# A hybrid-trunk step on one core: triangular inverse moved to POOL, pooling branch moved, state kept undecayed

## The chip, the cores and the metric

The kernel runs on one core of a Trainium2 chip. The metric is device time in microseconds (us) of one execution. The median of three executions of the kernel before is 1899.89 us (1899.71 to 1901.06).

The engines are named as in the profile: PE multiplies matrices (PEld is its weight load), DVE is the vector engine, ACT the scalar engine with its activation tables, POOL the third elementwise engine, whose queue also issues DMAs. SP issues DMAs.

## The reference, cut to what matters

One layer of a trunk, for 256 prompt tokens and 64 sample tokens together (NT = 320):

```
proj = rmsnorm(x) @ w_in            -> u_pool | u_rwkv | g_pool | g_rwkv
A = pool_mixer(u_pool)              # trailing means of 2/4/8/16 tokens minus the token, one 256x256 map for each of 4 groups, a scale
B = rwkv7_mix(u_rwkv, S0)           # token shift, then for each of 16 heads a state S (64 x 64), token by token:
    S = S*w_t + (S @ -kk_t) b_t^T + v_t k_t^T ;  y_t = S @ r_t
x += (sigmoid(g_pool)*(A @ proj_pool) + sigmoid(g_rwkv)*(B @ proj_rwkv)) @ w_out
x += SwiGLU(rmsnorm(x));   x += sigmoid(rmsnorm(x) @ w_ple_gate) * (p @ w_ple_proj);   final rmsnorm
```

It also returns the last row before the shift, the last 15 pooling rows and the final states S.

## The kernel before, in words

**Layout.** Channels lie on the 128 partitions, the 320 tokens along the free axis. Every weight product is made in three float32r products (`mm3`, L111: high times high, high times low, low times high). `unit` (L91) brings eight 128x128 weight tiles: SP loads `raw`, ACT casts it to `wh` (L98), DVE subtracts to `wl` (L100; its rows show L56, the line of the helper `TT`). The three tags have three slots each. `gemm` (L103) runs through units; its accumulators `acc` have two PSUM banks.

**Order.** The program is written in one order, and a planner sets the order of each engine's queue when the kernel is built, by priorities and its own estimates of durations; on the chip every queue runs in that fixed order. Weight units have a raised priority (L94).

**Stages.** At the start (L189 to L336) come the small projection `pp`, the first norm and three narrow tiles (`low`, L289). Then come four groups (`group`, L423), one for every four heads, and after each group some `fill`s (L171): gemms that no group needs (the pooling input `d_u` and the gates `d_gate`, sent to DRAM). `FILLS` (L38) gives 5, 4, 4 and 22 of the 40. They are what PE has to do while a group's chain of small steps runs. After the last group comes the pooling branch (`pool_load`, `pool_diff`, `pool_mix`, L341 to L383), five more fills (L714), `acc_pa` (A times proj_pool), and then `acc_pb`, `acc_o`, the feed-forward `acc_fg`, `acc_fu` and `acc_fd`, `acc_pg` and the final norm.

**One group.** Six gemms `acc_q`, each shifted by a token (`shift`, L159): DVE multiplies into `rp`, in which every chunk of 64 tokens has a column ahead of it; two copies on POOL (L161, L162) fill that column, a third (L163) keeps the last row, ACT scales, DVE adds. The six tiles are scaled by accumulated decays into `ar` and `bk`; keys are normalized by `rsqrt_tp` (L693: Sqrt on ACT, reciprocal on DVE, a Newton step). Products of `bk` and `ar`, masked, are `mg`. For every chunk and head the kernel needs the inverse of a 64x64 unit triangular matrix. Its two 32x32 diagonal blocks, for all chunks and heads, go through DRAM (`dF`) into `xb`, 40 blocks on 40 partitions, and are inverted by 30 steps of two DVE instructions (L565 to L569):

```
for s in range(1, 31):
    n = 31 - s
    mul(tm, xb[:, 0:s, s:s + 1].broadcast_to([40, s, n]), xb[:, s:s + 1, s + 1:32].broadcast_to([40, s, n]))
    TT(xb[:, 0:s, s + 1:32], xb[:, 0:s, s + 1:32], tm, ALU.add)
```

DVE adds 1 on the diagonal, ACT makes a transposed copy `xbt` of 20 blocks (L572), both go through DRAM into `X` and `tz`, and PE makes the block below the diagonal (`pz`, `px`). Then the chunks go in four rounds (L621): PE reads the state (`ra`, L613), applies `X` (`pu`), makes the chunk's contribution `ps_s` (L642); DVE adds the old state and multiplies by the chunk's decay `pcs` (L651, L653), which gives `sbd`, the state that the next round's `ra` reads. Group norm and gate follow (L666 to L691), and the result goes to DRAM (`d_yb`).

Of the kernel before, what the change touches and what calls it, by code (L numbers as in the profile page):

```python
# [13 lines left out]
ALU = mybir.AluOpType  # L14
# [23 lines left out]
FILLS = (5, 4, 4, 22)  # L38
# [10 lines left out]
def trunk_step(ctx: ExitStack, tc: tile.TileContext, xT, pT, cols, w_low, s0T, poolpast, cst, maskc, invc,  # L49
# [139 lines left out]
    with tc.tile_pool(name="start", bufs=1) as st:  # L189
# [99 lines left out]
        def low(q, a=None):  # L289
            rp = st.tile([P, NCH, C + 1], F32, tag="rp", name="rp0", bufs=2)  # L290
            xs = xstd.rearrange("p (c t) -> p c t", c=NCH)
# [6 lines left out]
            ac = a.rearrange("p (c t) -> p c t", c=NCH)  # L298
            if q == 2:
# [38 lines left out]

    ZL = PAST + T_P + PAST + T_S
# [10 lines left out]
    def pool_diff(gi, z):  # L350
# [12 lines left out]
        t16 = rk.tile([P, 2, 16], F32, tag="tm", name="t16")  # L363
# [10 lines left out]
    def pool_mix(gi, dh, dl):  # L374
        h, l = unit(w_poolw[gi], 4, f"pw{gi}")
        for i in range(2):
# [5 lines left out]
            act.activation(yah[:, j, :], a, AF.Copy, scale=col(C_PS + j))  # L382
            stt(yal[j], a, col(C_PS + j), f(yah[:, j, :]), ALU.mult, ALU.subtract)  # L383
# [9 lines left out]
    with tc.tile_pool(name="rk", bufs=1) as rk:  # L393

        def shift_tile(q, out):
# [27 lines left out]
        def group(g):  # L423
# [109 lines left out]

            bt = rk.tile([P, 2 * NCH, P], F32, tag="bt", name="bt")
# [68 lines left out]
            sbd_in = rk.tile([P, 2, P], F32, tag="sbd", name="sbd_in", bufs=4)  # L603
# [16 lines left out]
            states = {4: sbd_in, 0: None}  # L620
            for cs in ((4, 0), (1,), (2,), (3,)):  # L621
# [326 lines left out]
```

## Time and profile before

| | us |
|---|---|
| median of three executions | 1899.89 |
| the profiled execution, its own time | 1900.61 |
| its span, first to last instruction | 1898.7 |
| PE busy in the span | 1863.8 |
| DVE / ACT / POOL busy | 1120.1 / 798.6 / 138.7 |
| mean granted clock of PE | 0.993 of full speed |

The span and what lies around it (1.9 us) make the execution's own time. A clock of 1.00 is 2.4 GHz, of 0.50 is 1.2 GHz. Busy time doesn't say what an engine waited for: the views of the rows below do.

### The profile page before, as it was taken

What the parts mean: (1) busy time and instruction counts of PE and PEld (TensorE: products, weight loads), DVE (VectorE), ACT (ScalarE), POOL (GpSimd) and SP (SyncE); (2) the same over time, 40 slices, a digit from 0 to 9 for tenths busy, and PEclk for the clock granted to TensorE, in tenths of its full rate; (3) what the DMA queues carried; (4) which work ended last, traced back from release to release, by engine and by line L of the source; (5) the groups of instructions that cost most, each with busy time, mean ns of one, the idle gap of its engine ahead of it and who ended that gap; (6) DMA issues with size and microseconds to landing.
All of it is one profiled execution on the core that took longest, in us unless ns stands there. A gap on an engine that the chain in (4) does not pass through costs nothing.

```text
span 1898.7 us, 32757 instructions
## 1 busy us (share of the span) xinstructions
PE 1863.8 (98%) x13444; PEld 1838.0 (97%) x13444; DVE 1120.1 (59%) x1674; ACT 798.6 (42%) x1060; POOL 138.7 (7%) x282
## 2 busy tenths in 40 slices
PE   8999999899999999999999999999999999999997
PEld 7999999799989999999999999999999999999997
DVE  7676976877857465555454554444545554445655
ACT  6554536464455334443333333223333333333543
POOL 0110222202310112000000000000000000000000
PEclk9999999899999999999999999999999999999998
DMA  7554544345545657444444444554444444555553
GB/s 274 168 170 150 167 147 148 105 161 181 169 138 189 199 191 233 146 152 148 151 150 149 152 147 148 146 151 156 153 146 154 146 154 143 152 146 150 169 170 117
DMA packets 95349, 302.99 MB, mean 160 GB/s; under 512 B 12224, under 2 KB 23248, under 8 KB 95200
## 3 DMA queue, kind: packets, MB, share of 16 engines
q1 hardware_dynamic: 78336, 271.71, 44.3%
q0 software_dynamic: 6816, 17.39, 3.0%
q10 hardware_dynamic: 10048, 11.80, 1.7%
q8 instruction: 106, 1.74, 0.4%
q14 instruction: 43, 0.35, 0.1%
HBM read 284.12 MB, written 16.73 MB: 158 GB/s over the span
## 4 chain that ended last, share of the span: by engine, by line
PE 95%; DVE 3%; DMA 1%; issue 1%; ACT 0%; SPq 0%; DVEq 0%; ACTq 0%
PE acc_fd L115 5%; PE acc_fu L116 5%; PE acc_fg L116 5%; PE acc_fg L115 5%; PE acc_fg L117 5%; PE acc_fu L117 5%; PE acc_fd L116 5%; PE acc_fu L115 5%; PE acc_fd L117 5%; PE acc_f L115 4%; PE acc_f L116 4%; PE acc_f L117 4%; PE acc_q L117 3%; PE acc_q L115 3%; PE acc_q L116 3%; PE acc_pg L115 2%
## 5 line engine op out<-in xcount | busy, mean ns | idle before, releaser
L116 PE MATMUL acc_fg<-nl,wh_fg 128*128 128x320 f32 x704 | 217.8, 309 | 0.0
L115 PE MATMUL acc_fg<-nh,wh_fg 128*128 128x320 f32 x704 | 217.6, 309 | 0.1
L115 PE MATMUL acc_fu<-nh,wh_fu 128*128 128x320 f32 x704 | 217.5, 309 | 0.0
L117 PE MATMUL acc_fu<-nh,wl_fu 128*128 128x320 f32 x704 | 217.5, 309 | 0.0
L116 PE MATMUL acc_fu<-nl,wh_fu 128*128 128x320 f32 x704 | 217.5, 309 | 0.0
L117 PE MATMUL acc_fg<-nh,wl_fg 128*128 128x320 f32 x704 | 217.5, 309 | 0.0
L56 DVE TENSOR_TENSOR wl_fd<-raw_fd,wh_fd 128x1024 fp32r<-128x1024 f32 (+1 forms) x96 | 109.1, 1136 | 151.7 <-ACT wh_fd L98 151.7
L98 ACT CAST wh_fd<-raw_fd 128x1024 fp32r<-128x1024 f32 (+1 forms) x96 | 94.1, 980 | 203.1 <-PE acc_fd L116 162.4
L98 ACT CAST wh_fg<-raw_fg 128x1024 fp32r<-128x1024 f32 x88 | 92.5, 1051 | 199.1 <-PE acc_fg L116 98.7
L98 ACT CAST wh_fu<-raw_fu 128x1024 fp32r<-128x1024 f32 x88 | 92.5, 1052 | 190.8 <-PE acc_fu L116 103.4
L56 DVE TENSOR_TENSOR wl_fg<-raw_fg,wh_fg 128x1024 fp32r<-128x1024 f32 x88 | 107.8, 1225 | 105.3 <-ACT wh_fg L98 105.3
L115 PE MATMUL acc_f<-xh,wh_f 128*128 128x320 f32 x512 | 160.8, 314 | 1.7 <-ACT wh_f L98 1.7
L116 PE MATMUL acc_f<-xl,wh_f 128*128 128x320 f32 x512 | 160.6, 314 | 0.0
L117 PE MATMUL acc_f<-xh,wl_f 128*128 128x320 f32 x512 | 159.5, 312 | 0.8 <-DVE wl_f L56 0.8
L115 PE MATMUL acc_fd<-hh,wh_fd 128*128 128x320 f32 x512 | 158.2, 309 | 0.0
L116 PE MATMUL acc_fd<-hl,wh_fd 128*128 128x320 f32 x512 | 158.2, 309 | 0.0
L117 PE MATMUL acc_fd<-hh,wl_fd 128*128 128x320 f32 x512 | 158.2, 309 | 0.0
L56 DVE TENSOR_TENSOR wl_fu<-raw_fu,wh_fu 128x1024 fp32r<-128x1024 f32 x88 | 107.8, 1226 | 83.9 <-ACT wh_fu L98 83.9
L115 PEld LDWEIGHTS acc_fg<-nh,wh_fg 128*128 128x128 f32 x704 | 132.2, 188 | 0.3 <-issue 0.3
L116 PEld LDWEIGHTS acc_fg<-nl,wh_fg 128*128 128x128 f32 x704 | 132.2, 188 | 0.1
L117 PEld LDWEIGHTS acc_fg<-nh,wl_fg 128*128 128x128 f32 x704 | 132.2, 188 | 0.1
L116 PEld LDWEIGHTS acc_fu<-nl,wh_fu 128*128 128x128 f32 x704 | 132.2, 188 | 0.0
(490 smaller groups left out, 4913.0 us busy)
## 6 DMA issues: line engine op xcount, KB each, us to landing
raw_fg<-in_w_gate SPq DMA_DIRECT2D x88, 512.0 KB, 3.7
raw_fu<-in_w_up SPq DMA_DIRECT2D x88, 512.0 KB, 3.7
raw_f<-in_w_in SPq DMA_DIRECT2D x64, 512.0 KB, 4.0
raw_fd<-in_w_down SPq DMA_DIRECT2D x64, 512.0 KB, 3.6
raw_q<-in_w_in SPq DMA_DIRECT2D x48, 512.0 KB, 3.9
raw_o<-in_w_out SPq DMA_DIRECT2D x32, 512.0 KB, 3.7
raw_pg<-in_w_pg SPq DMA_DIRECT2D x32, 512.0 KB, 3.9
raw_fd<-in_w_down SPq DMA_DIRECT2D x32, 384.0 KB, 3.5
```

The source lines that it names most:

```text
L56: return vec.tensor_tensor(out=out, in0=a, in1=b, op=op)
L98: act.copy(h, raw)
L115: pe.matmul(out=acc, lhsT=hs[i], rhs=xh, start=first and i == 0, stop=False)
L116: pe.matmul(out=acc, lhsT=hs[i], rhs=xl, start=False, stop=False)
L117: pe.matmul(out=acc, lhsT=ls[i], rhs=xh, start=False, stop=last and i == n - 1)
```

## The change

- **Inverse.** The 60 instructions of a group's inverse, the diagonal and the transposed copy go to POOL.
- **Pooling.** It is written directly behind the last group and ahead of its fills, of which there are now 27 (none is left for afterwards). Its weights no longer go through `unit`: POOL loads them into slots of the tag `tp`. Its output goes to DRAM (`d_ya`) and is read back by POOL, cast by ACT and split by DVE ahead of `acc_pa`.
- **Shift.** `rp` has no column ahead of a chunk; the two copies on POOL go, and a second, two-column DVE instruction makes the first token of either request.
- **Undecayed state.** The next round reads the state without `pcs`; `ar` of chunks 1 to 3 carries it instead (one POOL instruction for a group, `later`). DVE multiplies by `pcs` into `dec`, which the next round's addition reads.
- **Log norms.** In `rsqrt_tp` the reciprocal becomes Ln and Exp on ACT.
- **Start and end.** The four first matmuls on zeros write `acc` banks; the last norm's factor comes by another formula, one DVE instruction shorter; the output goes in nine pieces, the first two half as large.

```diff
-FILLS = (5, 4, 4, 22)
+FILLS = (5, 4, 4, 27)
...
     def shift(q, rp, t, out):
-        pool.tensor_copy(out=rp[:, 0:5:4, 0], in_=ssz[:, q, :])
-        pool.tensor_copy(out=rp[:, 1:4, 0], in_=rp[:, 0:3, C])
-        pool.tensor_copy(out=nshift[:, q, :], in_=rp[:, 3:5, C])
-        act.activation(t, rp[:, :, 1:], AF.Copy, scale=omu[:, q:q + 1])
-        stt(out.rearrange("p (c t) -> p c t", c=NCH), rp[:, :, 0:C], col(C_MU + q), t, ALU.mult, ALU.add)
+        pool.tensor_copy(out=nshift[:, q, :], in_=rp[:, T_P - 1:NT:T_S])
+        act.activation(t, rp, AF.Copy, scale=omu[:, q:q + 1])
+        stt(out[:, 1:], rp[:, 0:NT - 1], col(C_MU + q), t[:, 1:], ALU.mult, ALU.add)
+        stt(out[:, 0:T_P + 1:T_P], ssz[:, q, :], col(C_MU + q), t[:, 0:T_P + 1:T_P], ALU.mult, ALU.add)
...
-            w = small("warm_ps", [P, NT])
+            w = acc_tile("warm_ps")
...
     def pool_mix(gi, dh, dl):
-        h, l = unit(w_poolw[gi], 4, f"pw{gi}")
+        raw = rf.tile([P, 4 * P], F32, tag="tp", name="raw_pw", bufs=6)
+        pool.dma_start(out=raw, in_=w_poolw[gi])
+        h = rf.tile([P, 4 * P], F32R, tag="tp", name="wh_pw", bufs=6)
+        act.copy(h, raw)
+        l = rf.tile([P, 4 * P], F32R, tag="tp", name="wl_pw", bufs=6)
+        TT(l, raw, f(h), ALU.subtract)
...
-            act.activation(yah[:, j, :], a, AF.Copy, scale=col(C_PS + j))
-            stt(yal[j], a, col(C_PS + j), f(yah[:, j, :]), ALU.mult, ALU.subtract)
+            o = sp.tile([P, NT], F32, tag="gate", name="pool_o", bufs=2)
+            act.activation(o, a, AF.Copy, scale=col(C_PS + j))
+            act.dma_start(out=d_ya[j], in_=o)
...
+            later = ar[:, :, 1:4].rearrange("p j c s t -> p j c (s t)")
+            pool.tensor_tensor(out=later, in0=later, in1=pcs[:, :, 0:3].unsqueeze(3).broadcast_to([P, 2, 3, P]),
+                               op=ALU.mult)
...
-                mul(tm, xb[:, 0:s, s:s + 1].broadcast_to([40, s, n]), xb[:, s:s + 1, s + 1:32].broadcast_to([40, s, n]))
-                TT(xb[:, 0:s, s + 1:32], xb[:, 0:s, s + 1:32], tm, ALU.add)
+                pool.tensor_tensor(out=tm, in0=xb[:, 0:s, s:s + 1].broadcast_to([40, s, n]),
+                                   in1=xb[:, s:s + 1, s + 1:32].broadcast_to([40, s, n]), op=ALU.mult)
+                pool.tensor_tensor(out=xb[:, 0:s, s + 1:32], in0=xb[:, 0:s, s + 1:32], in1=tm, op=ALU.add)
...
-            vec.tensor_scalar(out=diag, in0=diag, scalar1=1.0, scalar2=None, op0=ALU.add)
-            act.copy(xbt, xb[0:20].rearrange("u s t -> u t s"))
+            pool.tensor_scalar(out=diag, in0=diag, scalar1=1.0, scalar2=None, op0=ALU.add)
+            pool.tensor_copy(out=xbt, in_=xb[0:20].rearrange("u s t -> u t s"))
...
-                    for lo in halves:
-                        src = ps[lo, i]
-                        if states[c] is not None:
-                            TT(nxt[lo, :, lo], src, states[c][lo, :, lo], ALU.add)
-                            src = nxt[lo, :, lo]
-                        mul(nxt[lo, :, lo], src, pcs[lo, :, c:c + 1].broadcast_to([64, 2, C]))
+                    for lo, new_s in zip(halves, at):
+                        if states[c] is None:
+                            vec.tensor_copy(out=new_s, in_=ps[lo, i])
+                        else:
+                            old = sbd_in[lo, :, lo] if c == 4 else dec[c][lo]
+                            TT(new_s, ps[lo, i], old, ALU.add)
                     new[c] = nxt
+                    for lo, new_s in zip(halves, at):
+                        mul(dec[c + 1][lo], new_s, pcs[lo, :, c:c + 1].broadcast_to([64, 2, C]))
...
             act.activation(s, am, AF.Sqrt)
+            act.activation(s, s, AF.Ln)
             r = tp("r")
-            vec.reciprocal(out=r, in_=s)
+            act.activation(r, s, AF.Exp, scale=-1.0)
...
             group(g)
+            if g == 3:
+                for gi in range(4):
+                    pool_mix(gi, *pool_diff(gi, pool_load(gi)))
             fill(n)
...
-        for gi in range(4):
-            pool_mix(gi, *pool_diff(gi, pool_load(gi)))
+        for j in range(8):
+            yt = sp.tile([P, NT], F32, tag="gate", name="ya", bufs=2)
+            pool.dma_start(out=yt, in_=d_ya[j])
+            act.copy(yah[:, j, :], yt)
+            TT(yal[j], yt, f(yah[:, j, :]), ALU.subtract)
```

## Rows read from the trace of the kernel before

**Rows 1.** The page's first part: busy time, share of the span, instructions.

```profile
PE 1863.8 (98%) x13444; PEld 1838.0 (97%) x13444; DVE 1120.1 (59%) x1674; ACT 798.6 (42%) x1060; POOL 138.7 (7%) x282
```

**Rows 2.** Stretches: length, busy PE, PEld, DVE, ACT, POOL, granted clock, DMA share, GB/s.

```profile
20.00:40.00 20.00, 15.78 (x98) 14.10 (x96) 17.61 (x26) 12.31 (x21) 0.00 (x0) 1.00 0.82 278
...
340.00:360.00 20.00, 12.46 (x115) 11.41 (x115) 19.18 (x33) 7.43 (x14) 5.25 (x12) 0.74 0.35 109
...
349.00:360.00 11.00, 6.33 (x53) 5.92 (x54) 10.38 (x20) 3.18 (x7) 3.68 (x9) 0.53 0.21 73
...
556.00:578.00 22.00, 16.30 (x166) 13.50 (x166) 18.54 (x37) 10.24 (x21) 4.91 (x8) 1.00 0.34 106
...
578.00:582.00 4.00, 4.00 (x18) 4.00 (x19) 3.65 (x11) 2.64 (x5) 0.00 (x0) 0.57 0.47 154
```

**Rows 3.** Timeline around the first stall: start, duration, instruction, idle before and its releaser.

```profile
337.49 4.15 DVE L697 RECIPROCAL r<-s 128x640 f32<-128x640 f32 x1 [2.14 <-ACT s L695]
...
347.63 0.44 PE L613 MATMUL ra<-sbd,ar 128*64 128x128 f32 x4 [2.21 <-DVE sbd L56]
...
352.12 0.61 DVE L56 TENSOR_TENSOR sbd<-ps_s,sbd 64x128 f32<-64x128 f32 x2
...
354.89 0.60 DVE L56 TENSOR_TENSOR sbd<-sbd,pcs 64x128 f32<-64x128 f32 x2
...
355.63 0.69 PE L613 MATMUL ra<-sbd,ar 128*64 128x128 f32 x4 [4.20 <-DVE sbd L56]
```

**Rows 4.** Timeline around the second stall, SP's queue and PE.

```profile
535.71 13.89 SPq L96 DMA_DIRECT2D raw_pw<-in_w_poolw  x4
...
565.56 0.44 PE L613 MATMUL ra<-sbd,ar 128*64 128x128 f32 x4 [0.97 <-DVE sbd L56]
...
568.41 0.41 PE L115 MATMUL acc_f<-xh,wh_f 128*128 128x320 f32 x1 [0.61 <-ACT wh_f L98]
...
575.41 0.42 PE L115 MATMUL acc_f<-xh,wh_f 128*128 128x320 f32 x1 [1.11 <-ACT wh_f L98]
...
577.85 0.41 PE L117 MATMUL acc_f<-xh,wl_f 128*128 128x320 f32 x1 [0.75 <-DVE wl_f L56]
```

**Rows 5.** Groups of DVE instructions: busy in all, mean ns, idle before.

```profile
L56 DVE TENSOR_TENSOR tm<-xb 40x30 f32<-40x30 f32 (+14 forms) x120 | 38.3, 319 | 11.4 <-DMA xb<-dF 8.8
...
L697 DVE RECIPROCAL r<-s 128x640 f32<-128x640 f32 x4 | 16.6, 4149 | 3.6 <-ACT s L695 3.6
```

**Rows 6.** Stretches that hold the inverses of groups 1 and 3, tile xb alone: DVE, ACT, POOL.

```profile
257.00:295.00 38.00, 19.36 (x61) 1.24 (x1) 0.54 (x1) 1.00 0.42 137
...
467.00:509.00 42.00, 19.42 (x61) 1.93 (x1) 1.07 (x2) 1.00 0.45 143
```

**Rows 7.** POOL by groups, and POOL beside DVE in the timeline.

```profile
L161 POOL COPY rp<-ssz 128x2 f32<-128x2 f32 x27 | 16.0, 596 | 11.2 <-DVE ssz L267 4.8 <-DVE xv L62 2.9 <-DVE xb L56 2.2
L542 POOL MEMSET uv<- 64x1280 f32 x4 | 4.7, 1165 | 6.2 <-PE py_c L617 3.6 <-PE acc_q L117 2.5
...
219.47 3.94 POOL L161 COPY rp<-ssz 128x2 f32<-128x2 f32 x1
...
222.15 1.21 DVE L56 TENSOR_TENSOR wl_q<-raw_q,wh_q 128x1024 fp32r<-128x1024 f32 x1
223.57 0.60 DVE L62 SCALAR_TENSOR_TENSOR xr<-rp,ct,tsh 128x320 f32<-128x320 f32 x1 [0.21 <-POOL rp L162]
...
223.63 0.18 POOL L161 COPY rp<-ssz 128x2 f32<-128x2 f32 x1
```

**Rows 8.** Groups of ACT instructions.

```profile
L695 ACT ACT_TABLE_LOAD x4 | 5.1, 1283 | 2.9 <-DVE am L485 2.9
```

**Rows 9.** Timeline at the end, DVE.

```profile
1888.70 5.94 DVE L56 TENSOR_TENSOR X<-X,r_fin 128x640 f32<-128x640 f32 x8 [1.30 <-PE r_fin L859]
```

**Rows 10.** Tile acc_pa: duration min/median/max in ns, first and last start in us.

```profile
L115 PE MATMUL acc_pa<-yah,wh_pa x128: 306/308/314, 613.2 to 669.1; 128*128 128x320 f32 x128
```

**Rows 11.** DMA issues: number, KB each, median us from issue to landing.

```profile
gate<-d_gate POOLq DMA_DIRECT2D x32, 160.0 KB, 3.2
```

More of the change, by code (lines that the diff above doesn't have):

```diff
@@ L289, in low @@
         def low(q, a=None):
-            rp = st.tile([P, NCH, C + 1], F32, tag="rp", name="rp0", bufs=2)
-            xs = xstd.rearrange("p (c t) -> p c t", c=NCH)
+            rp = st.tile([P, NT], F32, tag="rp", name="rp0", bufs=2)
             if a is None:
@@ L297, in low @@
                     gemm(a, w_in[q], KD, f"t{q}", xs_in)
-            ac = a.rearrange("p (c t) -> p c t", c=NCH)
             if q == 2:
@@ L302, in low @@
                     act.copy(r3[32 * i:32 * i + 32], a[96:128])
-                TT(rp[0:96, :, 1:], ac[0:96], r3[0:96].rearrange("p (c t) -> p c t", c=NCH), ALU.add)
-                mul(rp[0:96, :, 1:], rp[0:96, :, 1:], xs[0:96])
-                mul(rp[96:128, :, 1:], ac[96:128], xs[96:128])
-            else:
-                mul(rp[:, :, 1:], ac, xs)
-            t = st.tile([P, NCH, C], F32, tag="tsh", name="tsh0", bufs=2)
+                TT(rp[0:96], a[0:96], r3[0:96], ALU.add)
+                mul(rp[0:96], rp[0:96], xstd[0:96])
+                mul(rp[96:128], a[96:128], xstd[96:128])
+            else:
+                mul(rp, a, xstd)
+            t = st.tile([P, NT], F32, tag="tsh", name="tsh0", bufs=2)
             out = st.tile([P, NT], F32, tag="xm0", name="xm0", bufs=2)
@@ L336, in trunk_step @@
         TT(t2s[64:96], t2[64:96], f(t2s[64:96]), ALU.subtract)
+    d_ya = dr.tile([8, P, NT], F32, name="d_ya")
     ZL = PAST + T_P + PAST + T_S
@@ L362, in pool_diff @@
         a, b = PAST, 2 * PAST + T_P
-        t16 = rk.tile([P, 2, 16], F32, tag="tm", name="t16")
+        t16 = rk.tile([P, 2, 16], F32, tag="t16", name="t16")
         mul(t16, cur[:, :, a:a + 16], iv[:, gi:gi + 1, :].broadcast_to([P, 2, 16]))
@@ L398, in shift_tile @@
             gemm(a, w_in[q], KD, f"q{q}", xs_in)
-            rp = rf.tile([P, NCH, C + 1], F32, tag="rp", name="rp", bufs=3)
-            mul(rp[:, :, 1:], a.rearrange("p (c t) -> p c t", c=NCH), xstd.rearrange("p (c t) -> p c t", c=NCH))
-            t = rf.tile([P, NCH, C], F32, tag="tsh", name="tsh", bufs=2)
+            rp = rf.tile([P, NT], F32, tag="rp", name="rp", bufs=3)
+            mul(rp, a, xstd)
+            t = rf.tile([P, NT], F32, tag="tsh", name="tsh", bufs=2)
             shift(q, rp, t, out)
@@ L602, in group @@
             ysb = rk.tile([P, NCH, 2, C], F32, tag="ysb", name="ysb")
-            sbd_in = rk.tile([P, 2, P], F32, tag="sbd", name="sbd_in", bufs=4)
+            sbd_in = rk.tile([P, 2, P], F32, tag="sbd", name="sbd_in", bufs=3)
             pool.memset(sbd_in, 0.0)
@@ L620, in group @@
             states = {4: sbd_in, 0: None}
+            dec = {}
             for cs in ((4, 0), (1,), (2,), (3,)):
@@ L851, in trunk_step @@
                       stop=src is sql and i == 2)
-    rc = fp.tile([P, 3], F32, name="rc")
-    rsqrt(fp, s, c_eps, [P, 3], "rsc", 3, rc)
+    rc = [fp.tile([P, 3], F32, tag="rsc", name="rsc", bufs=4) for _ in range(4)]
+    act.activation(rc[0], s, AF.Sqrt, bias=c_eps)
+    vec.reciprocal(out=rc[1], in_=rc[0])
+    stt(rc[2], s, c_eps, rc[1], ALU.add, ALU.mult)
+    TT(rc[2], rc[2], rc[0], ALU.add)
+    vec.reciprocal(out=rc[3], in_=rc[2])
     rr = small("r_fin", [P, 1, NT])
@@ L857, in trunk_step @@
         dg = fp.tile([P, P], F32, tag="dg", name="dg", bufs=3)
-        vec.tensor_scalar(out=dg, in0=ident, scalar1=rc[:, i:i + 1], scalar2=None, op0=ALU.mult)
+        vec.tensor_scalar(out=dg, in0=ident, scalar1=rc[3][:, i:i + 1], scalar2=2.0, op0=ALU.mult, op1=ALU.mult)
         pe.matmul(out=rr[:, 0, lo:t + P], lhsT=one_sq, rhs=dg[:, lo - t:], start=True, stop=True)
-    for m in range(0, KD, 2):
-        mul(X2[:, m:m + 2, :], X2[:, m:m + 2, :], rr.broadcast_to([P, 2, NT]))
-        nc.sync.dma_start(out=o_y[:, m:m + 2, :], in_=X2[:, m:m + 2, :])
+    for m, n in ((0, 1), (1, 1), (2, 2), (4, 2), (6, 2), (8, 2), (10, 2), (12, 2), (14, 2)):
+        mul(X2[:, m:m + n, :], X2[:, m:m + n, :], rr.broadcast_to([P, n, NT]))
+        nc.sync.dma_start(out=o_y[:, m:m + n, :], in_=X2[:, m:m + n, :])
 def kernel(**inputs):
```

13 lines of the change are left out of this document (10 added, 3 removed).

## The prediction

> **What bounds the kernel now.** The page's first part comes first: PE is busy in 98% of the span and every other engine in at most 59% [rows 1]. An edit that leaves PE's instructions alone, as this one does, can gain only where PE stands still or runs slowly. The table by stretches shows where: apart from the start and the end there are two places. From 340 to 360 PE is busy for 12.46 of 20 us, so it idles 7.5; in 349 to 360 its granted clock averages 0.53, so the 6.33 us that it was busy there held some 3.0 us too many. From 556 to 578 it idles 5.7, and in 578 to 582 its clock is 0.57, which costs another 1.7 [rows 2]. Together that is 17.9 us, 0.9% of the time, and nearly all that the middle of the kernel can give.
>
> The timeline says what ends these waits. In the first stall PE waits for the state: `ra` stands behind DVE for 2.21 and 4.20 us [rows 3]. A chain of two DVE steps leads there, the addition at 352.12 and the multiplication by the decay at 354.89; DVE is not slow in them, it has other work between and is busy for 19.18 of the 20 us [rows 2, 3]. Part of that backlog is a reciprocal of 4.15 us just before [rows 3]. In the second stall PE waits for the weights of fills, 0.61, 1.11 and 0.75 us, and again for the state, 0.97 [rows 4]. The weights are late because four pooling units, asked for by SP from 535.71 on [rows 4], lie in the three weight slots until their pooling tiles are ready.
>
> **The change, part by part.**
>
> *Undecayed state.* The multiplication leaves the way to `ra`. In the long wait PE could start when the addition ends, 352.12 + 0.61 = 352.73, and not at 355.63: 2.8 us. The short wait of 2.21 loses between the multiplications' own 0.6 and all of it; I take 1.4. The 0.97 of the second stall goes: 1.0. The instruction `later` on POOL has 768 elements on a partition. POOL's nearest row is a memset of 1280 elements in 1.165 us, 0.91 ns each [rows 7]: 0.7 us for one pass, 2.1 if its two reads and its write come in turn, hidden behind the inverse's DMAs, which PE's state reads wait for anyway; exposed, at most 4 x 2.1 = 8.4.
>
> *Inverse off DVE.* 120 pairs leave DVE; one half took 38.3 us [rows 5], so both about 77, and with the reciprocals' 16.6 DVE is rid of 93 us in the stretch of the groups. What it is worth is only the backlog: the first stall's idle time less the two waits above, 7.5 - 2.8 - 1.4 = 3.3. I take half, 1.6; the ends are 0 and 3.3.
>
> *Inverse on POOL.* No row shows a POOL tensor_tensor. A step has on average the sum of s(31 - s) over 30 steps, 4960, divided by 30: 165 elements. A POOL copy of two elements takes 0.18 us undisturbed [rows 7], one pass over 165 elements by the memset 0.15. Low end: 0.18 + 0.15 = 0.33 us. High end: three passes, and every instruction waits as the copies L161 do on average (596 ns less 0.18): 0.18 + 0.45 + 0.42 = 1.05 us. Why they wait is plain at 219.47: a copy of two elements takes 3.94 us, DVE's subtraction from 222.15 on ends at 223.36, and the copy ends at 223.41 [rows 7]. I take two passes and half the wait, 0.18 + 0.30 + 0.21 = 0.69, because DVE will be emptier by 93 us. So an inverse takes 60 x 0.69 = 41 us, within 20 and 63. On DVE, between other work, it took at most 38 and 42 us in groups 1 and 3 [rows 6], and longer in groups 0 and 2. It is then no later than before, and fills cover it as they did. For what comes late I charge 1.5 us (ends 0 and 46, below).
>
> The Trainium skill has a rule against this part: the page SBUF — State Buffer, section Who interferes with whom, says that a DVE instruction with two SBUF inputs and a POOL instruction that reads SBUF exclude each other, and that the one that starts first holds the port for its whole length. The trace agrees for one direction, the copy of 3.94 us [rows 7]; for the other it has only a DVE wait of 0.21 us for a POOL copy that it needed [rows 7]. By that rule the term would be no gain from DVE's freed time, which is the second rival.
>
> *Queued behind the inverse on POOL:* the `nshift` copies, the loads of the gate, of `X` and `tz`, the states' stores, and the pooling's loads. A held `nshift` holds one of three `rp` buffers and then DVE and an `acc` bank; that costs PE only if POOL lets nothing through for the time of some five gemms. I count 0; if the cover goes, it is part of the slower case.
>
> *Transposed copy and diagonal.* 1024 elements in a row on POOL: one pass 0.9, two 1.9 us, plus a wait; ACT loses as much. The chain is as long as before: 0.
>
> *Shift.* 27 times two POOL copies go (L161 alone 16.0 us [rows 7]); 27 small DVE instructions come, each at most the 319 ns of an inverse step [rows 5], below 9 us in all, on an engine that gets 93 back: 0.
>
> *Log norms.* 4.15 us of DVE give way to two passes of ACT, each a fifth of that or less by the 0.74 us of a 128x640 DVE pass (5.94 for eight [rows 9]), and one or two table loads of 1.28 [rows 8]: 2.8 to 4.0 us. The chain is not longer, and the ACT time, at most 16 us, is under PE's gemms: 0.
>
> *The pooling branch* keeps its arithmetic, but its weights no longer take the fills' slots. The three waits go, 0.61 + 1.11 + 0.75 = 2.5 us. It gains a way through DRAM: eight stores, eight loads by POOL, eight casts and subtractions. Fills run until `acc_pa` starts at 613.2 [rows 10], so this is covered as long as the pooling ends some 20 us earlier; if not, see the third rival.
>
> *Clock.* In both stalls the clock fell to the lower level, 1.2 GHz, only behind several us of idle PE. If the waits shrink as above, 3.0 + 1.7 = 4.7 us come back; if half of them stay, none.
>
> *Start and end.* At the start DVE is busy for 17.61 of 20 us and ACT for 12.31 [rows 2]; the edits there take nothing off either: 0, within 1.3 either way. At the end one DVE instruction of about 0.2 goes, and the first store starts some 0.3 earlier because its multiplication is half as long (0.37 for 0.74 [rows 9]), one more piece is issued: -0.3, within -0.5 and +0.3.
>
> **The sum.** First stall 2.8 + 1.4 + 1.6 + 3.0 = 8.8; second 1.0 + 2.5 + 1.7 = 5.2; end 0.3; charged 1.5. The gain is 12.8 us on the profiled execution's 1900.6: 1887.8, rounded to 1888. That execution is 0.7 above the median of the runs shown, within what I round. This case's own range is 1883 to 1895.
>
> **The rivals.**
>
> 1. *POOL's inverse comes late, and PE stands before it (slower).* The place is `pz`, the first matmul that needs the inverse. PE's queue has a fixed order, so when POOL is slower than the planner thought, the gemms behind `pz` wait too. The price: at 0.90 us a step (two passes, the full mean wait) an inverse takes 54 us, 16 more than the 38 of group 1 and 12 more than the 42 of group 3 [rows 6]. 28 us against 14.3 gained: 1900.6 - 14.3 + 28 = 1914. It decides from (38 + 42 + 14.3) / 120 = 0.79 us a step. At the high end of 1.05 an inverse takes 63, 46 late in all, and the time is 1932. For it speaks that a POOL copy can wait 3.94 us; against it, that much of DVE's load is what goes away, and that groups 0 and 2 lived with longer inverses without a PE wait for them. The Trainium skill's GPSIMD Engine Reference, section Elementwise — side-by-side cycle accounting, measures a tensor_tensor there at 1.96 times DVE's time; by that estimate a step is 0.63 us, short of this point.
>
> 2. *The port gives DVE nothing back (the inverse moved in name only).* 240 steps of 0.69 are 166 us in which DVE's two-input work must wait, more than the 93 freed. The backlog stays and the clock falls again. What is left is 2.8 + 1.4 + 1.0 + 2.5 + 0.3 less 1.5: 6.5, so 1894. If the two waits for the state also come back behind other queued work, it is 1898.
>
> 3. *The pooling output comes late (no change).* The last fills end before `acc_pa` has its input. POOL's loads stand behind group 3's inverse, and with two buffers the eight loads go in four rounds of about 3.2 us [rows 11] and two passes of at most 0.74 [rows 9]: 4 x 4.7 = 19 us. If 13 of them lie open, it eats the gain: 1900.
>
> 4. *All of both stalls goes.* 7.5 + 3.0 + 5.7 + 1.7 + 0.5 = 18.4: 1882.
>
> **How the numbers follow.** Forecast 0.50; rival 1 0.21; rival 2 0.10, half of it on either side of the bound; rival 3 0.09; rival 4 0.10. A difference below 0.2%, 3.8 us, can hardly be told from none: faster is below 1896.1, slower above 1903.7. Faster 0.50 + 0.10 + 0.05 = 0.65; same 0.09 + 0.05 = 0.14; slower 0.21. The range reaches from 1879, somewhat below rival 4 (the start's 1.3 and a little), to 1910; it takes in rivals 2 to 4 and the lower part of rival 1, and leaves out the rest of it, some 0.14.
>
> **What would show it.** Right: no PE wait of over 1 us for `ra` behind DVE, no wait of fills for `wh_f` around the pooling, PE's clock at 1.00 throughout the groups, POOL's steps at 0.5 to 0.8 us from start to start, DVE some 90 us less busy. Wrong: PE waits for `pz` or `px` behind `tz` and `X` (rival 1); DVE's wl subtractions longer than 1.2 us and the first stall still there (rival 2); idle PE right before `acc_pa` (rival 3). A gain at the start or the end of more than 1.5 us would show a term that I set at nothing.

## The result, and the profile after

The changed kernel takes 1918.93 us in the median (1916.8 to 1920.03), the kernel before beside it 1900.43: a ratio of 1.0094, with a 95% interval of 1.0082 to 1.0107. It is slower by 18.5 us. The profiled execution of the changed kernel took 1918.91 us with a span of 1917.1, 18.4 us more than the span before. The page's first part:

```profile
PE 1869.1 (97%) x13444; PEld 1843.6 (96%) x13444; DVE 1077.1 (56%) x1461; ACT 811.1 (42%) x1083; POOL 311.4 (16%) x484
```

Against [rows 1] PE is busy 5.3 us longer and idle 13.1 us longer (1917.1 - 1869.1 = 48.0, before 1898.7 - 1863.8 = 34.9): together the 18.4 us. DVE is 43 us less busy, not 90. The waits of PE (line waited for, releaser; us in total, times, longest) name a wait that was not there before:

```profile
PE pz L596 <- DMA tzz<-dT: 15.3, 3, 7.1
PE acc_pw L115 <- ACT wh_pw L376: 4.0, 1, 4.0
```

The waits for `ra` of [rows 3, 4] are gone, and those of the fills too. The stretches (columns as in [rows 2]) show both stalls of before filled, and where the time went instead:

```profile
220.00:240.00 20.00, 13.93 (x157) 13.25 (x156) 9.39 (x14) 5.28 (x9) 4.98 (x7) 0.74 0.41 123
320.00:340.00 20.00, 12.88 (x151) 12.05 (x150) 7.82 (x10) 12.38 (x18) 4.09 (x8) 0.74 0.38 118
340.00:360.00 20.00, 20.00 (x194) 18.52 (x194) 15.90 (x29) 7.34 (x13) 2.56 (x6) 1.00 0.34 109
440.00:460.00 20.00, 17.89 (x245) 16.43 (x245) 16.75 (x28) 9.91 (x18) 6.84 (x12) 0.91 0.70 205
520.00:540.00 20.00, 16.02 (x99) 15.75 (x98) 10.50 (x15) 7.25 (x10) 15.53 (x29) 0.91 0.71 207
560.00:580.00 20.00, 20.00 (x195) 18.70 (x194) 12.60 (x26) 8.92 (x16) 2.64 (x5) 1.00 0.48 149
```

The four largest new stalls stand in place of two; over the stretches of the first two the granted clock averages 0.74. The timeline gives the first three their name. PE waits for the transposed inverse, in groups 0, 1 and 2:

```profile
228.79 1.28 PE L596 MATMUL pz<-tzz,mg 32*32 32x32 f32 x40 [6.07 <-DMA tzz<-dT]
...
329.03 1.28 PE L596 MATMUL pz<-tzz,mg 32*32 32x32 f32 x40 [7.12 <-DMA tzz<-dT]
...
443.29 0.82 PE L596 MATMUL pz<-tzz,mg 32*32 32x32 f32 x40 [2.11 <-DMA tzz<-dT]
```

One would say: POOL is slower than DVE. The tile `tm`, by which each of the four inverses can be followed (number; duration min/median/max in ns; first and last start in us), shows that this is only a part of it. First the kernel before, groups 0 to 3:

```profile
L56 DVE TENSOR_TENSOR tm<-xb x30: 182/342/401, 166.5 to 233.9; 40x30 f32<-40x30 f32 x2, 40x58 f32<-40x58 f32 x2, 40x84 f32<-40x84 f32 x2, 40x108 f32<-40x108 f32 x2
L56 DVE TENSOR_TENSOR tm<-xb x30: 183/338/401, 258.0 to 292.6; 40x30 f32<-40x30 f32 x2, 40x58 f32<-40x58 f32 x2, 40x84 f32<-40x84 f32 x2, 40x108 f32<-40x108 f32 x2
L56 DVE TENSOR_TENSOR tm<-xb x30: 182/324/399, 389.2 to 452.6; 40x30 f32<-40x30 f32 x2, 40x58 f32<-40x58 f32 x2, 40x84 f32<-40x84 f32 x2, 40x108 f32<-40x108 f32 x2
L56 DVE TENSOR_TENSOR tm<-xb x30: 182/342/400, 471.2 to 506.1; 40x30 f32<-40x30 f32 x2, 40x58 f32<-40x58 f32 x2, 40x84 f32<-40x84 f32 x2, 40x108 f32<-40x108 f32 x2
```

And the changed kernel:

```profile
L576 POOL TENSOR_TENSOR tm<-xb x30: 320/569/1634, 166.4 to 214.0; 40x30 f32<-40x30 f32 x2, 40x58 f32<-40x58 f32 x2, 40x84 f32<-40x84 f32 x2, 40x108 f32<-40x108 f32 x2
L576 POOL TENSOR_TENSOR tm<-xb x30: 250/599/1689, 263.7 to 317.0; 40x30 f32<-40x30 f32 x2, 40x58 f32<-40x58 f32 x2, 40x84 f32<-40x84 f32 x2, 40x108 f32<-40x108 f32 x2
L576 POOL TENSOR_TENSOR tm<-xb x30: 247/552/1602, 378.6 to 430.4; 40x30 f32<-40x30 f32 x2, 40x58 f32<-40x58 f32 x2, 40x84 f32<-40x84 f32 x2, 40x108 f32<-40x108 f32 x2
L576 POOL TENSOR_TENSOR tm<-xb x30: 226/568/1437, 475.6 to 524.0; 40x30 f32<-40x30 f32 x2, 40x58 f32<-40x58 f32 x2, 40x84 f32<-40x84 f32 x2, 40x108 f32<-40x108 f32 x2
```

From first to last start DVE took 67.4, 34.6, 63.4 and 34.9 us, 200 in all; POOL takes 47.6, 53.3, 51.8 and 48.4, 201 in all. So in groups 1 and 3 the inverse is 19 and 14 us longer than on DVE, in groups 0 and 2 it is 20 and 12 us *shorter*. Yet in group 0 PE now waits 6.07 us, where it waited for nothing. What also differs is PE's own queue. Counted in the two kernels' orders, between a group's last masked product and its `pz` there stood 552, 322, 529 and 335 gemm matmuls before, and 409, 398, 414 and 452 now. One takes 0.147 us from start to start, so the cover was 81, 47, 78 and 49 us and is 60, 59, 61 and 66. The order is set when the kernel is built; the planner's estimates are not on record, only the order that came of them.

Both sides together give the waits. In us from the start of a group's last masked product, to the landing of `tz` (the transposed inverse, `tzz` in the rows) and to PE's arrival at `pz`:

| group | `tz` there, before / now | PE at `pz`, before / now | PE waits now |
|---|---|---|---|
| 0 | 87.5 / 73.4 | 89.9 / 67.3 | 6.1 |
| 1 | 57.0 / 76.7 | 59.7 / 69.6 | 7.1 |
| 2 | 86.6 / 74.5 | 87.6 / 72.4 | 2.1 |
| 3 | 57.8 / 74.0 | 62.7 / 81.5 | none |

In groups 0 and 2 PE comes sooner by more than the inverse does; in group 1 the inverse comes later by more than PE. In group 0 the way out grew as well. These are the loads of `tz` there, before and after:

```profile
241.63 0.68 POOL L583 DMA_DIRECT2D tzz<-dT  x1
...
223.89 0.68 POOL L592 DMA_DIRECT2D tzz<-dT  x1
```

They landed 2.3 and 4.9 us after their issue, so from the start of the last step (233.9 and 214.0) to the landing it was 10.0 us and is 14.8. In groups 1 and 2 it went from 11.6 to 11.9 and from 11.6 to 12.9.

The last new stall, in 520 to 540, is the wait for `acc_pw`. The timeline shows its weights: POOL issues their load only near the end of group 3's inverse, behind which it was queued.

```profile
521.16 0.61 POOL L374 DMA_DIRECT2D raw_pw<-in_w_poolw  x1
...
525.53 0.42 PE L115 MATMUL acc_pw<-dh,wh_pw 128*128 128x320 f32 x1 [3.98 <-ACT wh_pw L376]
```

The groups of instructions (busy in all, mean ns of one, idle before) give the price of the steps, and what DVE paid:

```profile
L576 POOL TENSOR_TENSOR tm<-xb 40x30 f32<-40x30 f32 (+14 forms) x120 | 85.4, 712 | 19.8 <-DMA xb<-dF 11.2
L578 POOL TENSOR_TENSOR xb<-xb,tm 40x30 f32<-40x30 f32 (+14 forms) x120 | 83.7, 697 | 8.3
...
L56 DVE TENSOR_TENSOR wl_q<-raw_q,wh_q 128x1024 fp32r<-128x1024 f32 x48 | 62.3, 1298 | 38.4 <-ACT wh_q L98 38.2
```

A step's instruction is busy for 705 ns in the mean; the 60 of an inverse, with what POOL does between them, take 49.2, 53.9, 52.4 and 49.1 us to the end of the last one, 0.85 us each. DVE's subtraction for `wl_q` went from 1219 to 1298 ns in the mean.

### The profile page after: what moved, and what is told of

Same layout as the page of the kernel before. It is cut to its first block, busy times and chain, and to the rows that moved or that the text cites. A ratio compares the mean times of both kernels' runs of the same rounds, so it can differ in the third digit from the quotient of the medians.

```text
span 1917.1 us, 32767 instructions
## 1 busy us (share of the span) xinstructions
PE 1869.1 (97%) x13444; PEld 1843.6 (96%) x13444; DVE 1077.1 (56%) x1461; ACT 811.1 (42%) x1083; POOL 311.4 (16%) x484
## 4 chain that ended last, share of the span: by engine, by line
PE 81%; POOL 10%; DMA 3%; issue 2%; DVE 1%; ACT 1%; SPq 0%; ACTq 0%; DVEq 0%; POOLq 0%
PE acc_fd L116 5%; PE acc_fg L115 5%; PE acc_fg L117 5%; PE acc_fu L117 5%; PE acc_fu L115 5%; PE acc_fu L116 5%; PE acc_fg L116 5%; PE acc_fd L117 5%; PE acc_fd L115 5%; POOL tm L576 4%; POOL xb L578 4%; PE acc_pg L117 2%; PE acc_o L116 2%; PE acc_o L115 2%; PE acc_pg L116 2%
## 5 line engine op out<-in xcount | busy, mean ns | idle before, releaser
L854 POOL DMA_DIRECT2D pp<-d_pp x16 | 8.6, 538 | 1117.9 <-DVE gt L56 1117.1
```

Of the source, the lines that this page charges most:

```text
L854: pool.dma_start(out=pp, in_=d_pp[m])
```

## The experiments

Medians and ratios go against runs of the kernel before on the same chip (1899.85 to 1900.96 us in the median).

| run | what | us | ratio, 95% interval |
|---|---|---|---|
| e2_inv_only | before + inverse part | 1923.63 | 1.0121 [1.0106, 1.0136] |
| e4_micro | the steps by themselves, another program, one run | 256.15 | none |
| e5_pool_move | before + pooling move | 1906.7 | 1.003 [1.0018, 1.0042] |
| e7_undecayed | before + undecayed state | 1899.73 | 0.9996 [0.9987, 1.0005] |
| e10_log_norms | before + log norms | 1900.49 | 0.9998 [0.9988, 1.0007] |
| e1_inv_back | change - inverse part | 1907.69 | 1.0042 [1.0025, 1.0059] |
| e6_pool_back | change - inverse part - pooling move | 1904.69 | 1.0024 [1.0015, 1.0034] |
| e3_half | change, half the steps on DVE | 1901.64 | 1.0004 [0.9995, 1.0013] |
| e8_pz_late | change, `pz` later, spread | 1924.38 | 1.0122 [1.0107, 1.0137] |
| e9_pz_block | change, `pz` later in groups 0, 1 | 1912.34 | 1.0066 [1.0052, 1.0079] |
| e13_pz_all | change, `pz` later in all groups | 1904.73 | 1.0022 [1.0013, 1.0032] |
| e11_pool_early | before + pooling beside group 2 | 1895.88 | 0.9976 [0.9968, 0.9985] |
| e12_half_pool_early | e3_half + pooling beside group 2 | 1904.84 | 1.0024 [1.0015, 1.0033] |
| e14_no_inv_pool_early | e1_inv_back + pooling beside group 2 | 1898.41 | 1.0 [0.9987, 1.0013] |
| e15_early_undecayed | e11_pool_early + undecayed state | 1896.89 | 0.9987 [0.9978, 0.9996] |

### The inverse part alone, undone, and halved

```
e1 (on the change), e2 the other way round (on the kernel before):
-  pool.tensor_tensor(out=tm, ...); pool.tensor_tensor(out=xb[...], ...)
+  mul(tm, ...); TT(xb[...], ...)
-  pool.tensor_scalar(out=diag, ...); pool.tensor_copy(out=xbt, ...)
+  vec.tensor_scalar(out=diag, ...); act.copy(xbt, ...)
e3 (on the change): steps s <= 15 on POOL, the others, diag and xbt as in e1
```

> The changed kernel with the 60 steps of a group's inverse and the diagonal back on DVE and the transposed copy back on ACT; all other parts of the change stay. Theory (the inverse on POOL is ready later than PE's fixed order allows, so PE stands before pz in every group): the four waits for pz go, and what the other parts gain stays: 1883 to 1893 us. Rival (the loss comes from other parts: the pooling's loads on POOL's queue, the table loads of the log norms, a longer DVE): it stays above 1905 us.

> The kernel before with only the inverse, the diagonal and the transposed copy moved to POOL. Theory: PE waits for pz in most groups, and the time is 1912 to 1930 us, since the stalls of before are not mended either. Rival (other parts carry the loss): 1890 to 1903 us.

> The changed kernel with steps 1 to 15 of the inverse on POOL, steps 16 to 30 and the diagonal on DVE, the transposed copy on ACT. Theory: an inverse spends some 25 us on POOL and under 20 on DVE, PE's wait for pz falls to under 3 us a group, 1885 to 1900 us. Rival (the loss is not from the length of POOL's part): the same 1915 to 1921 us as the changed kernel.

The inverse part alone costs more than the whole change, 22.7 us (1923.63 against 1900.96). PE's waits in it:

```profile
PE pz L588 <- DMA tzz<-dT: 18.4, 3, 9.1
PE acc_f L115 <- ACT wh_f L98: 6.0, 3, 4.3
```

Its `pz` stands behind 399, 409, 414 and 452 gemm matmuls, nearly the cover of the changed kernel: the planner moves `pz` when the inverse alone becomes POOL's. With the inverse back (e1) the change is 11 us faster, but still 6.7 slower than before; the 1883 to 1893 that the theory gave were missed. There PE waits elsewhere:

```profile
PE acc_pa L115 <- ACT yah L738: 5.8, 4, 3.0
PE pz L595 <- DMA tzz<-dT: 2.8, 1, 2.8
```

So a second part costs something once the first is gone. Half the steps on each engine (e3) bring the time to that of before, just outside the expected 1885 to 1900, with one `pz` wait of 1.6 us left.

### The steps by themselves

> Not the computation: it only runs the 60 steps on POOL on zeros six times: alone, beside back-to-back DVE subtractions with two SBUF operands (128x1024), alone, beside such with one operand in PSUM, alone, beside DVE subtractions alternating with DVE reductions; the outputs are zeros. Theory (DVE's two-operand instructions keep POOL from reading): 33 to 42 us alone, 50 us or more beside the first kind until DVE is done, as alone beside the second, in between beside the third; DVE's subtractions get longer than 1.23 us only beside the first and the third kind. Rival (POOL is slow by itself): about 50 us in all six.

The six inverses did not meet DVE's work as planned: it ran beside the first three, and the last three ran alone. That answers the question too. The stretches are the first four inverses (length; busy DVE; busy POOL; clock; DMA); the last two are as the fourth:

```profile
7.30:67.60 60.30, 58.31 (x46) 55.62 (x60) 1.00 0.14 50
67.60:105.70 38.10, 37.04 (x33) 33.40 (x60) 1.00 0.00 0
105.70:150.90 45.20, 33.27 (x26) 40.44 (x61) 1.00 0.00 0
150.90:185.40 34.50, 0.00 (x0) 29.79 (x61) 1.00 0.00 0
```

Alone an inverse takes 34.5 us, 0.575 a step. The first three met mixtures, so the steps tell more. While subtractions of two SBUF tiles ran one after the other (11.7 to 57.5 us), POOL came through 30 steps, 1.53 us each from start to start, and a subtraction took 1.49 in the mean. Beside the same subtraction with one operand in PSUM, 18 steps of the same inverse took 0.52 each and 47 of the next 0.61, and the subtraction stayed at 1.22. The third inverse met alternating subtractions and one-input reductions for most of its time and took 45 us.

In the changed kernel an inverse takes 49 to 54. Its 240 instructions can be sorted by what DVE ran beside them: 74 beside nothing took 0.437 us in the mean (the same ones alone in e4: 0.434), 76 beside a weight subtraction 1.04 (alone 0.535), 90 beside other work of DVE 0.64 (alone 0.507). Of the 50.7 us by which all are longer than alone, 38.6 fall to those beside a weight subtraction. The Trainium skill's page SBUF — State Buffer, section Who interferes with whom, has the rule for this (a DVE instruction with two SBUF inputs and a POOL instruction that reads SBUF exclude each other); these runs agree, for both directions, with the 1.53 and 0.52 us of a step and the 1.49 and 1.22 of a subtraction.

### `pz` later in PE's order

```
e8:
+      with tc.high_priority(offset=(-1450, -1450, -1600, -1300)[g]):
           for u in range(10): for jj in range(2): pe.matmul(out=pz[...], ...)
e9, ahead of that loop, which stays as in the change:
+      for jj in range(2):
+          with tc.high_priority(offset=(-1500, -1450, -1650, -1300)[g]):
+              pe.matmul(out=pz[64 * jj + 32:64 * jj + 64], lhsT=mgu[0:32, 0, 32:64], rhs=tz[0:32, 0:10, :], ...)
e13: as e9, offset=(-1480, -1460, -1750, -1400)[g]
```

> The changed kernel with the pz matmuls given a lower priority, so that the planner puts them later in PE's fixed order: the gemm matmuls between a group's last masked product and pz become 449, 471, 389 and 506 instead of 409, 398, 414 and 452 (at 0.145 us: +5.8, +10.6, -3.6 and +7.8 us of cover). Nothing else is edited. Theory A (the loss is PE's fixed order, which meets an inverse that POOL makes later than the planner thought): the pz waits of 6.1 and 7.1 us in groups 0 and 1 shrink below 1.5 us, the one of group 2 grows from 2.1 to about 5.7, the clock stays up in groups 0 and 1; 8 to 13 us faster than the change, 1906 to 1911. Theory B (the loss is contention: DVE's longer subtractions hold the weights back, and pz is only where it shows): the time stays above 1914, and waits for weights or chain steps take the place of those for pz.

> The changed kernel with pz kept in one block but later in PE's fixed order: two extra matmuls that write the pz tile first, at a lower priority, and are overwritten by the real ones, hold the block back. Between a group's last masked product and pz stand 459, 449, 404 and 464 gemm matmuls instead of 409, 398, 414 and 452, at 0.145 us each +7.2, +7.4, -1.4 and +1.7 us of cover. Theory A (the loss is the place of pz in PE's order before an inverse that comes late): the waits of 6.1 and 7.1 us in groups 0 and 1 go, the one of group 2 grows from 2.1 to about 3.5, and the clock stays up behind the first two; 10 to 18 us faster than the change, 1901 to 1909. Theory B (the loss is contention between POOL and DVE, which another place of pz only moves): above 1912, with waits for weights or for chain steps in place of those for pz.

> The changed kernel with pz held back in all four groups, in the same way as with pz in one block: 439, 444, 527 and 512 gemm matmuls between a group's last product and pz instead of 409, 398, 414 and 452, which is +4.3, +6.7, +16.4 and +8.7 us of cover. Theory A (place in PE's order is the whole loss): at most one pz wait of some 2 us is left, in group 0, the clock stays at 1.00 from 200 to 600, and the time comes to 1900 to 1905. Theory B (the chain behind pz is then late too: a round, the next group and the pooling start later and PE runs out of gemms elsewhere): pz waits under 2 us, but new waits of 5 us or more behind pz, around the pooling or at the end of the groups, and 1908 to 1916.

In e8 the idle time of PE goes as theory A has it (1924.9 - 1889.1 = 35.8 us; the change has 48.0), but PE is busy 20 us longer: with a low priority for each small matmul, the planner put them by twos between the gemm matmuls, and that is slow in itself (last section). So e8 decides nothing. In e9 the block stays whole. The stretches of groups 0 and 1 are full or nearly so, at clock 1.00; that of group 2 is not:

```profile
220.00:240.00 20.00, 20.00 (x246) 18.44 (x245) 14.77 (x20) 7.24 (x13) 7.56 (x9) 1.00 0.55 176
320.00:340.00 20.00, 19.57 (x250) 17.71 (x249) 13.78 (x20) 15.41 (x24) 1.24 (x2) 1.00 0.28 96
420.00:440.00 20.00, 9.13 (x90) 7.89 (x88) 15.71 (x20) 6.28 (x8) 13.51 (x19) 0.76 0.67 189
```

The waits of 6.07 and 7.12 us went, by 50 matmuls each; the one of group 2, left with 404, grew from 2.11 to 9.9, where I expected 3.5: PE came 2.7 us sooner than in the change, but `tz` also landed 5 us later, 79.5 us after the last product. So the count of matmuls alone doesn't fix the wait. That missed the time (1912.34, expected 1901 to 1909; theory B had above 1912) and left the question open. e13 gives cover to all four. There `tz` lands 73, 75, 73 and 77 us after a group's last product, about as in the change, and PE comes to `pz` after 74, 80, 92 and 95. No `pz` wait is left, and the longest wait is now for the pooling's weights:

```profile
PE acc_pw L115 <- ACT wh_pw L376: 5.8, 1, 5.8
```

The time is 1904.73, within the 1900 to 1905 of theory A, though the clock isn't at 1.00 throughout (0.91 from 220 to 240, 0.87 from 540 to 560). Against its own runs of the kernel before e13 is 4.9 us slower, the change 18.5: some 14 us come back with POOL's 240 instructions still on POOL, by a later `pz` in PE's order. The longest wait that is left is for the load queued behind the inverse:

```profile
532.10 0.58 POOL L374 DMA_DIRECT2D raw_pw<-in_w_poolw  x1
...
539.45 0.63 PE L115 MATMUL acc_pw<-dh,wh_pw 128*128 128x320 f32 x1 [5.80 <-ACT wh_pw L376]
```

### The pooling move alone, and earlier

```
e5: the kernel before with FILLS = (5, 4, 4, 27), own weight loads in pool_mix, d_ya, loads of ya
    (all as in the change); e6: e1 with these parts as before
e11, e12, e14, on e5, e3 and e1:
-            if g == 3:
+            if g == 2:
                 for gi in range(4): pool_mix(gi, *pool_diff(gi, pool_load(gi)))
```

> The kernel before with the pooling move alone (own weight loads on POOL, outputs through DRAM, fills 27). Theory A (the pooling output now comes late, as the 5.8 us that PE stood for the casts of the pooling output with the inverse back on DVE suggest): PE stands 4 to 8 us before the first acc_pa gemm and runs the next slice at a lower clock; the weight waits of 2.5 us in the second stall go; in all 3 to 8 us slower than before, 1904 to 1909. Theory B (the predicted term: the waits go and nothing comes in their place): 2 to 4 us faster, 1896 to 1899, no wait before acc_pa of over 1 us.

> The changed kernel with the inverse, diagonal and transposed copy back on DVE and ACT and the pooling branch back as it was before; the undecayed state, the shift, the log norms and the start and end stay. Theory A (inverse and pooling move are the two costs): faster than the kernel with the inverse alone undone (1907.7) by 10 us or more and faster than before by 4 to 10, 1890 to 1897; no waits for ra behind DVE of over 1 us. Theory B (something in the undecayed state, the shift or the norms costs): 1902 or more, with new waits inside the groups.

> The kernel before with the pooling move alone, but beside the third group instead of the last one: its input is complete after nine fills, so PE's order now has 891 gemm matmuls between the last pooling product and the first acc_pa gemm, where the move beside the last group alone had 40. Theory A (the pooling move cost 6 us only because its output came late): no wait before acc_pa, and the second stall, which the move had removed, stays away: 3 to 6 us faster than before, 1895 to 1898. Theory B (the move costs through the extra DMAs and casts wherever it stands): 1903 or more.

> The changed kernel with steps 1 to 15 of the inverse on POOL, steps 16 to 30, the diagonal and the transposed copy on DVE and ACT, and the pooling branch beside the third group. With half the steps the time was 1901.6 and no wait was above 2.2 us, so what is left are many small waits of 1 to 2 us. Theory A (each is a fixed-order wait that more gemms behind the last group shorten): 1 to 5 us faster than that, 1897 to 1901. Theory B (POOL and DVE slow each other wherever the pooling stands, and a third chain beside a group adds its DVE work where DVE is fullest): 1902 to 1907.

> The changed kernel without its inverse part (inverse, diagonal and transposed copy back on DVE and ACT) and with the pooling beside the third group: all the other parts of the change stay. If the two parts whose results come late were the only loss, the waits before acc_pa of 7.0 us go and it comes to 1893 to 1898, as the pooling move beside the third group alone (1895.9). If the shift, the log norms and the undecayed state together still cost by an earlier pz in the first group, 1899 to 1904 with a pz wait of 2 to 4 us from 230 to 245.

Alone (e5) the move costs 6.1 us. The second stall of before is wholly gone (560 to 580 is full), but the casts of the pooling output end after the last fill; waits, then stretches:

```profile
PE acc_pa L115 <- ACT yah L725: 7.1, 4, 3.5
```

```profile
560.00:580.00 20.00, 20.00 (x177) 18.77 (x177) 12.23 (x20) 8.88 (x16) 4.55 (x8) 1.00 0.57 171
...
600.00:620.00 20.00, 14.55 (x75) 13.21 (x73) 12.07 (x26) 10.41 (x20) 3.24 (x6) 0.76 0.72 236
```

The pooling needs the first eight fills and nothing else, so it can stand a group earlier. There (e11) 891 gemm matmuls lie between its last product and `acc_pa` instead of 40, the wait is gone, and the move gains: 1895.88, 4.5 us faster than before, with an interval clear of 1. That is the fastest median here. e6 fell on theory B's side: with both costly parts undone 4.1 us are still lost, and 4.7 us of PE's waits in it are for `pz`. On top of e6's parts the early pooling gains about what it gains alone: e14, all of the change but the inverse part, is 1.4 us faster than its runs of before where e6 is 4.1 slower, and so can't be told from before. It came out between its two ranges, with a `pz` wait of 3.8 us in group 0. On half the steps it does harm: e12 missed the expected 1897 to 1901 and is 3.2 slower than e3.

### The undecayed state and the log norms

```
e7: the kernel before with later, dec and sbd as in the change; e15: the same on e11
e10: the kernel before with Ln and Exp in rsqrt_tp
```

> The kernel before with the undecayed state alone. If the predicted term holds, the two waits for the state in the first stall and the one in the second go: 2.8 + 1.4 + 1.0 us and up to 4.7 us of clock, so 4 to 10 us faster, 1891 to 1897. Rival: DVE's backlog comes from the reciprocal and the inverse, so ra is ended by the addition, which is then late itself: waits for ra stay at more than half their length and the time is within 3 us of before.

> The kernel before with the log norms alone (reciprocal on DVE replaced by two passes on ACT). Theory A (the planner answers a shorter DVE with an earlier pz: in group 0 it now stands 19 gemm matmuls behind the first products of the next group, where before it stood behind the last): a pz wait of 1 to 4 us in group 0 and a time within 4 us above before, 1900 to 1905. Theory B (the predicted relief of DVE's backlog): the first stall from 340 to 360 loses 1.6 us or more and no wait comes in its place, 1895 to 1899.

> The kernel before with the pooling move beside the third group and the undecayed state. If the undecayed state only hands the wait for the state on to the next link of the chain, as it did alone (0.9996 of before), it is within 2 us of the pooling move alone, 1894 to 1898, with waits for pu behind ACT in place of those for ra. If it takes the waits of 6.7 us for ra that the pooling move left, 1888 to 1893.

The undecayed state alone gains nothing that can be told; the expected 1891 to 1897 were missed. PE's waits in it:

```profile
PE pu L638 <- ACT rhs L632: 4.1, 4, 1.9
PE ra L617 <- DVE sbd L56: 3.1, 3, 2.0
```

Before, `ra` waited 8.1 us in all and `pu` 0.7: five went at one link and 3.4 came at the next, since `rhs` was still late. On e11 it is the same again (1896.89 against 1895.88): `ra` waits 2.9 us where it waited 6.7, and `pu` 2.7. The log norms (e10) do what the prediction hoped of them: the stretch 340 to 360 is busy for 19.20 us where it was 12.46 [rows 2]. Yet the time stays, because the waits come back elsewhere:

```profile
240.00:260.00 20.00, 20.00 (x204) 18.28 (x204) 10.03 (x23) 7.70 (x14) 4.05 (x9) 0.74 0.34 101
340.00:360.00 20.00, 19.20 (x169) 17.95 (x167) 19.15 (x31) 10.59 (x18) 4.32 (x11) 1.00 0.35 119
440.00:460.00 20.00, 16.90 (x137) 15.62 (x136) 15.29 (x28) 7.25 (x8) 6.23 (x10) 0.98 0.64 191
```

The planner put group 0's `pz` ahead of the second batch of the next group's products, where before it stood among the last, and `pz` waits 4.1 us in three places. Its cover in group 0 is 502 gemm matmuls, as in e1 and e6 (552 before). So the `pz` wait that is left in those two probably comes from the log norms; no run takes them alone out of the change.

## Why the prediction was wrong

The forecast was 1888 and faster; it is 1919 and slower. Rival 1 happened in its place, `pz`. That the time lies near its price of 1914 is partly luck. It had POOL late in groups 1 and 3, by 16 and 12 us; PE waits 7.1 us in group 1, not at all in group 3, and 6.1 and 2.1 in groups 0 and 2, which it held safe. And it kept 14.3 us of gains, while the other parts without the inverse (e1) are slower than before.

**The step that failed** is "It is then no later than before, and fills cover it as they did", with 1.5 us charged. Its first half came true in groups 0 and 2 alone. In groups 1 and 3, the tight ones, an inverse was to take 41 us and takes 54 and 49, where DVE took 35 from first to last step. The second half took PE's queue for fixed, though the order of every queue is planned anew with each kernel: `pz` moved 17 to 21 us earlier in groups 0 and 2 (552 to 409, 529 to 414 matmuls). In group 1 the cover grew by 11 us (322 to 398), and POOL's inverse was 19 us longer than DVE's. What the runs show in place of the 1.5 is 15.3 us of waits for `pz`, and a lower clock behind two of them. e13 shows what this was worth: with a later `pz` some 14 us return.

**The price of a step** was right for the instruction: 0.69 us estimated, 0.705 busy, of which 0.49 is the instruction alone (e4) and 0.21 the wait beside DVE, both as estimated. What was left out is what lies between: start to start it is 0.85, beyond the 0.79 from which rival 1 decides. The estimate from the Trainium skill (GPSIMD Engine Reference, section Elementwise — side-by-side cycle accounting: 1.96 times DVE) gave 0.63; alone, a step measured 0.575 us from start to start and 0.49 busy, to DVE's 0.319 busy [rows 5]. It is near what POOL does alone, and too low beside DVE.

**Transposed copy and diagonal**, counted 0: on POOL they took 2.3 and 0.84 us in the mean, and in group 0 the way from the last step to `tz` became 4.8 us longer.

**Inverse off DVE.** 93 us were to leave; DVE's busy time fell by 43. By the groups of instructions some 8 of the missing 50 are the shift's small instructions, as charged; 10 are longer weight subtractions (`wl_q`, `wl_f`), as rival 2 said; 6 are eight small instructions of the group norm (last section); 6 more are the undecayed state's (20.5 us for `sbd` before, 26.3 for `sbd` and `dec` now), which the prediction did not count; the rest is spread thinly. That the backlog of the first stall was worth 1.6 us could not show: e10 removes most of that stall and gains nothing.

**Queue behind the inverse**, counted 0: the pooling's weight load waits there, 4.0 us in the change, 5.8 in e13.

**Undecayed state**, 2.8 + 1.4 + 1.0 us: the waits for `ra` did shrink, by 5.0, but the next link took 3.4 of it, and the time did not move (e7). "PE could start when the addition ends" was true of `ra`, not of the chain.

**The pooling branch**, 2.5 us: the three weight waits went, as said (e5 and the change are full from 560 to 580). The cover "as long as the pooling ends some 20 us earlier" was missing in e5 (rival 3), by 7.1 us. In the change itself it held, since there 307 gemm matmuls lie behind the last pooling product.

**Clock.** It was back at 1.00 where the old stalls went, and fell behind the new waits of 6 and 7 us. **Start and end**: near 0 as said; up to 200 us PE ran 1277 matmuls, before 1275, and from the last `acc_pg` matmul to the end it is 16.7 us in both.

## What to carry to other kernels

Where a planner orders the queues from its own estimates, a stage that gets a new engine is to be priced against the place where its consumer will then stand, not against the duration it had: count the covering instructions between producer and consumer in the new order. A stall that goes is a gain only if nothing later in the same chain, or in the next plan, takes its place; the undecayed state, the log norms and the pooling move each shrank the wait that it was aimed at, and only the pooling move gained, and that only a group earlier than it was put. In this kernel POOL's work beside DVE's made both slower, and a load that POOL issued behind that work came so late that PE stood for 4.0 to 5.8 us.

## What the hardware did that was not expected

POOL and DVE hold each other up in both directions, instruction by instruction. In the changed kernel's timeline the one that starts second is stretched:

```profile
272.32 0.51 POOL L576 TENSOR_TENSOR tm<-xb 40x184 f32<-40x184 f32 x1
272.33 1.57 DVE L56 TENSOR_TENSOR wl_f<-raw_f,wh_f 128x1024 fp32r<-128x1024 f32 x1
...
276.37 1.22 DVE L56 TENSOR_TENSOR wl_f<-raw_f,wh_f 128x1024 fp32r<-128x1024 f32 x1 [1.30 <-ACT wh_f L98]
276.41 1.64 POOL L578 TENSOR_TENSOR xb<-xb,tm 40x210 f32<-40x210 f32 x1
278.14 0.57 POOL L576 TENSOR_TENSOR tm<-xb 40x220 f32<-40x220 f32 x1
```

The subtraction that came second took 1.57 us, the one that came first 1.22; the POOL step beside the latter took 1.64, a larger one beside nothing 0.57. From 60 to 620 us the 37 weight subtractions that began while a POOL instruction ran took 1.45 us in the mean, the other 68 took 1.23. Small instructions pay too: the group norm's instruction on 10 elements for each partition, whose mean was 283 ns before, has this row now:

```profile
L689 DVE TENSOR_SCALAR mean<-mean 128x10 f32<-128x10 f32 x4 | 4.7, 1170 | 0.1
```

Two of the four make the mean, with 2.30 and 1.72 us; POOL instructions ran through nearly the whole of both. That POOL held them is read from this overlap; no run tries it alone.

And PE's clock fell here while the profile shows PE busy throughout. In e8 from 231.5 us on, two 32x32 matmuls alternated with one gemm matmul, 0.52 us for each three instead of about 0.2 (0.147 and twice 1.28 / 40). Stretches of 4 us, PE busy throughout:

```profile
228.00:232.00 4.00, 4.00 (x29) 3.60 (x27) 3.61 (x7) 1.51 (x2) 0.19 (x1) 1.00 0.53 192
232.00:236.00 4.00, 4.00 (x22) 2.50 (x21) 0.21 (x1) 0.41 (x1) 0.00 (x0) 0.81 0.34 124
236.00:240.00 4.00, 4.00 (x22) 2.73 (x23) 1.23 (x1) 0.63 (x1) 0.00 (x0) 0.50 0.24 79
```

The granted clock goes to 0.50, the lower level of 1.2 GHz, and PE's busy time in e8 is 20 us above that of the change. The same small matmuls in one block of 40 take 1.28 us in all.
